# Stage 1 of a hybrid mixer layer: wide products with tokens stationary, and what moves with them

## The chip, the cores and the metric

One NeuronCore of a Trainium2 chip runs one launch of the kernel; all weights and activations are float32 in HBM. The metric is the device time of the launch in microseconds; it is a median of runs. Engines are named TensorE (PE, its weight loads PEld), VectorE (DVE), ScalarE (ACT), GpSimd (POOL) and SyncE (SP).

## The reference

One layer (D = 4096, 256 latent tokens x, 256 context tokens):

```python
shift, scale, gate = split(silu(cvec) @ w_ada + b_ada, 3)     # for c and for c_ctx
h   = rmsnorm(x, norm_w) * (1 + scale) + shift                # x with c, ctx with c_ctx
q, k, v, ga, xl, gl = split(h @ w_in, SPLITS)                 # 2048, 512, 512, 2048, 2048, 2048 columns
att = attention(rope(rmsnorm(q)), rope(rmsnorm(k)), v)        # 16 query heads, 4 key/value heads
u   = conv4(xl) + conv_b
lru = scan_forward(u) + scan_backward(u)                      # context first, then latent tokens; 16 blocks
mix = [rmsnorm(att) * silu(ga), rmsnorm(lru) * silu(gl)]
out = x + gate * (mix @ w_out)                                # latent tokens only
```

Only the latent tokens leave the layer, so of the context just k, v and xl are needed.

## The kernel before, in words

Every large product is computed in three float32r products: an operand is split into a rounded part (hi) and the rest (lo), and hi x hi, hi x lo and lo x hi are summed in PSUM. The weights are split when they arrive: ScalarE copies the high part of a [128, 1024] tile (L640), VectorE subtracts it (L644). The contraction over D runs over 32 k-tiles of 128 rows.

Stage 1 (to about 757 us) makes k, v and xl for both streams. It goes over groups of k-tiles, of 1, 1, 2, 2, 2 and six times 4. For a group it needs shift and scale of the group's channels: `mod_tasks` multiplies silu(c) and silu(c_ctx) by w_ada. Most blocks of four rows go to TensorE (L483; the stationary operand is 32 columns wide, four products side by side in the array), some blocks to VectorE (L470, L472, one multiply-add per row and vector; TensorE folds their sum in, L495). `MOD_V = 6` of the 8 blocks of scale of a full group are on VectorE, none of shift; shift and scale have a bank and a row of their own (L502). `coeff_tasks` sums the row's partitions with products that have the row as stationary operand and two columns moving (L553). `prep_tasks` then transposes the group's tokens (L591), modulates them on ScalarE and splits them (L611).

The group's products follow. `kv_pieces` (L709 to L711) has 128 tokens stationary and 256 weight columns moving; `lru_pieces` (L740) has 128 weight columns stationary and 256 tokens moving, so that xl comes out with channels on partitions. A weight tile of a full group holds four k-tiles by 256 columns. Each filled PSUM bank (four in the pool `pm`) is added to a sum in SBUF by VectorE (L689; L687 for the first group). Per group there are 24 such additions of 512 columns.

Stage 2 makes q (L951 to L953, tokens stationary, 512 columns moving) and the attention, stage 3 the two gates (L975 to L977, weight columns stationary, 256 tokens moving), stage 4 the output projection (L951 to L953 again). Beside stages 2 and 3 the recurrence runs in 16 blocks of 128 channels: xl goes to DRAM after stage 1 (L930), POOL loads a block's gate weights and its xl (L1223, L1225), ScalarE and VectorE make the convolution (L1229, L1232), and gates and scans follow (L1255 to L1257, L1299). Scores, gates, coefficients and some transposes share two PSUM banks (`pe`).

The order of every engine's queue is fixed when the program is built: each piece of work is a task with estimated costs per engine, a due time `pos`, slots that it takes and gives back, and loads; `Plan.order` picks the task that can start first, the most urgent among equals. Engines run their queues in order. The loads of weight tiles go out on SP's queue in the order of their use, through six slots (`raw`).

Of the kernel before, what the change touches and what calls it, by code (L numbers as in the profile page):

```python
# [37 lines left out]
AHEAD = 16.8  # L38
LOAD = 1.500
# [4 lines left out]
QUADS = 1  # L44
LRU_CHUNKS = 10.2
MOD_V = 6
# [11 lines left out]
class Task:  # L58
    """A piece of the program: its engines and their estimated work, and what it waits for."""
# [19 lines left out]

class Plan:  # L80
    """Orders tasks for in-order engines: at each step the task that can start first, the most urgent among equals.
    Slots of the pools are counted, so that the order never needs a slot that is freed only later."""
# [44 lines left out]
    def fixed(self, tasks):  # L127
        """The first tasks, in the order given; their loads are issued as play() does."""
# [13 lines left out]
    def order(self):  # L142
        out, waiting = [], list(self.tasks)
        while waiting:
# [7 lines left out]
            # of the tasks that load, the most urgent of those that could start soon  # L152
# [23 lines left out]
    def put(self, t, s, dma):  # L176
# [6 lines left out]
        for e, c, *table in t.ops:  # L183
            # ScalarE's functions lie in tables, of which one is loaded
            if table and table[0] != self.table:
                self.table = table[0]
                c += TABLE
            s = max(s, self.t[e]) + c
            self.t[e] = s
            s += self.LAT  # L190
        t.end = s - self.LAT
        if t.ops[0][0] == "S":
            # a transfer: it ends later than its issue
            t.end = self.dma = max(self.dma, t.start + 1.3) + t.ops[0][1]
            self.t["S"] = t.start + 0.1
            t.end += 0.9
# [8 lines left out]
def kernel(  # L205
# [34 lines left out]
    SLOTS = dict(h4=(22, 1024), a8=(6, 2048), raw=(RAW, 1024), hi=(HL, 1024), lo=(HL, 1024), tp=(TP, 512), ta=(1, 512), td=(1, 512), wg=(2, 512),  # L240
                 xin=(1, 512), u=(1, 512), ga=(1, 512), ab=(2, 16), mx=(3, 2), ss=(5, 16), pm=(4, 512), pe=(2, 512), pt=(1, 512), po=(1, 512))
# [6 lines left out]
    def slot(cl, shape, dt=F32):  # L248
# [4 lines left out]
        if cl in ROUNDED:  # L253
            # float32r and float32 do not share a tile
# [26 lines left out]
    plan = Plan({cl: n for cl, (n, _) in SLOTS.items() if cl not in ("raw", "td", "ss")} | dict(lh=1, ah=3, lg=1), RAW)  # L281
# [28 lines left out]
    con = cp.tile([128, 130], F32, name="con")  # L310
    ident = con[:, 0:128]
    sel = con[:, 128:130]
# [7 lines left out]
    sc32 = [slot("wg", [128, KT // 2, 32]) for _ in range(2)]  # L320
# [5 lines left out]
    pick = cp.tile([128, 33], F32, name="pick")  # L326
    V.memset(pick, 0.0)
    V.memset(pick[:, 1:2], 1.0)
# [7 lines left out]
    for i in range(2):  # L336
        for v in range(2):
            V.tensor_copy(sc32[i][:, :, v], sc[:, v, KT // 2 * i : KT // 2 * i + KT // 2])
# [65 lines left out]
    def decay():  # L404
        # 4 softplus(-lam) = 4 max(-lam, 0) + 8 atanh(e / (2 + e)), e = exp(-|lam|)
# [18 lines left out]
    def rope_tasks(w, pos, after):  # L424
        """Rotary tables with the norm weights folded in: w * cos, and w with its halves swapped * (-sin | sin)."""
# [21 lines left out]
    def mod_tasks(k0, nk, out_, p0, p1, nb):  # L447
        """silu([c; c_ctx]) @ w_ada for shift and scale of nk k-tiles: partial sums on partitions 32q + vec of a
        row tile; those of some blocks of rows on VectorE, per vec on all partitions."""
# [3 lines left out]
        todo, ends = [], []  # L453
        for part, col0 in enumerate((128 * k0, D + 128 * k0)):
            on_v = MOD_V if part == 1 and nk == G else 0
            v_quads = [(quads * (2 * i + 1)) // (2 * on_v) for i in range(on_v)]
            p_quads = [q for q in range(quads) if q not in v_quads]
            src = w_ada[0, :, col0 : col0 + n].rearrange("(p k) n -> p k n", p=128)
            d = {}

            def on_vector(*w, k, v, first, d=d):
                if v == 0:
                    d["w"] = w[0]
                    if first:
                        d["acc"] = [slot(t, [128, n]) for t in ("xin", "u")]
                a = d["acc"][v]
                for i in range(step):
                    s_ = sc[:, v, k + i : k + i + 1]
                    if first and i == 0:
                        V.tensor_scalar_mul(a, d["w"][:, i], s_)  # L470
                    else:
                        V.scalar_tensor_tensor(out=a, in0=d["w"][:, i], scalar=s_, in1=a, op0=ALU.mult, op1=ALU.add)  # L472
                if v == 1:
                    drop(d["w"])

            cl = "pt" if part else "po"

            def on_tensor(*ws, k, d=d, p_quads=p_quads, cl=cl, on_v=on_v):
                if k == 4 * p_quads[0]:
                    d["ps"] = slot(cl, [128, n])  # L480
                for i in range(step * len(ws)):
                    quad, q = divmod(k + i, 4)
                    T.matmul(  # L483
                        d["ps"][32 * q : 32 * q + 32, :],
# [1048 lines left out]
```

## Time and profile before

| | |
|---|---|
| device time, median of 3 runs | 1804.12 us (1803.67 to 1807.31) |
| profiled execution, first to last instruction | 1805.1 us |
| TensorE / VectorE / ScalarE busy | 1752.0 / 1388.7 / 861.0 us |
| moved by DMA | 452.11 MB, 250 GB/s over the span |

The profiled execution has no other time of its own on record than its span. Busy time of TensorE counts a product from its start to its end, and products overlap: the distance between starts, not the duration of one, is what a product costs in a row of them. PEclk is the share of 2.4 GHz that was granted.

### The profile page before, as it was taken

The page shows a single profiled execution, that of the slowest core. Times are in us where ns is not written, and L with a number is a line of the kernel's source. Part 1 is how long each engine was busy: PE and PEld are TensorE (multiplying, and loading weights), DVE is VectorE, ACT ScalarE, POOL GpSimd, SP SyncE. Part 2 cuts the span into 40 slices and gives each one's busy share as a digit, 9 for nine tenths or more (in the row PEclk, how much of TensorE's full clock was granted, in tenths as well). Part 3 has the DMA queues.
Part 4 walks back from the last instruction along what each step waited for, and adds up shares of the span by engine and source line. Part 5 has one row for each costly group of instructions (what it writes and reads, how often), then busy time and mean ns, then how long its engine had stood idle before and what let it go on. Part 6 is the DMA issues. An engine that isn't in the chain of part 4 may idle for free.

```text
span 1805.1 us, 30493 instructions
## 1 busy us (share of the span) xinstructions
PE 1752.0 (97%) x12093; PEld 1527.8 (85%) x12093; DVE 1388.7 (77%) x1941; ACT 861.0 (48%) x1271; POOL 64.5 (4%) x111
## 2 busy tenths in 40 slices
PE   3999999999999999999999999999999999999998
PEld 2778879888989899977877889999999988888887
DVE  1565988787878797579788886877998997777774
ACT  4422222323232224247787876867776643333332
POOL 2000000000000000110000000000000000000000
PEclk9999999999999999999999999999999999999999
DMA  9989998788887885696555555556777699989883
GB/s 294 329 295 299 311 310 291 265 284 273 262 276 251 293 279 164 225 294 204 182 169 175 181 168 183 176 183 192 237 237 244 208 319 319 316 299 308 303 305 116
DMA packets 304782, 452.11 MB, mean 250 GB/s; under 512 B 15136, under 2 KB 159376, under 8 KB 304128
## 3 DMA queue, kind: packets, MB, share of 16 engines
q1 hardware_dynamic: 297824, 428.43, 71.9%
q0 software_dynamic: 6816, 21.74, 4.2%
q8 instruction: 95, 1.56, 0.4%
q14 instruction: 47, 0.39, 0.1%
HBM read 441.72 MB, written 8.39 MB: 249 GB/s over the span
## 4 chain that ended last, share of the span: by engine, by line
PE 49%; issue 42%; DVE 5%; ACT 2%; DMA 2%; POOL 0%; ACTq 0%; DVEq 0%; POOLq 0%
PE pm L952 8%; PE pm L953 8%; PE pm L951 8%; PE pm L977 6%; PE pm L975 6%; PE pm L976 6%; DVE lo L644 2%; PE po L1141 1%; PE pe L1255 1%; PE pe L1256 1%; PE pe L1257 1%; ACT hi L640 1%; PE pe L1103 1%; DMA rope<-in_q_norm_w_dram 1%; PE pt L1127 0%
## 5 line engine op out<-in xcount | busy, mean ns | idle before, releaser
L640 ACT CAST hi<-raw 128x1024 fp32r<-128x1024 f32 x416 | 434.8, 1047 | 694.9 <-PE pm L953 232.8
L644 DVE TENSOR_TENSOR lo<-raw,hi 128x1024 fp32r<-128x1024 f32 x416 | 506.1, 1221 | 147.7 <-ACT hi L640 140.9
L740 PE MATMUL pm<-h,hi 128*128 128x256 f32 x2048 | 338.8, 288 | 2.8 <-DVE a L689 2.8
L740 PEld LDWEIGHTS pm<-h,hi 128*128 128x128 f32 x2048 | 283.0, 193 | 35.8 <-issue 21.7
L951 PE MATMUL pm<-hi,h 128*128 128x512 f32 x768 | 308.4, 402 | 0.0
L952 PE MATMUL pm<-lo,h 128*128 128x512 f32 x768 | 299.8, 390 | 2.3 <-DVE lo L644 2.3
L953 PE MATMUL pm<-hi,h 128*128 128x512 f32 x768 | 300.2, 391 | 0.0
L975 PE MATMUL pm<-h,hi 128*128 128x256 f32 x1024 | 292.4, 286 | 0.0
L977 PE MATMUL pm<-h,lo 128*128 128x256 f32 x1024 | 289.8, 283 | 1.4 <-DVE lo L644 1.4
L976 PE MATMUL pm<-h,hi 128*128 128x256 f32 x1024 | 289.7, 283 | 0.0
L689 DVE TENSOR_TENSOR a<-pm,a 128x512 f32<-128x512 f32 x240 | 163.0, 687 | 109.0 <-PE pm L740 66.8
L740 PE MATMUL pm<-h,lo 128*128 128x256 f32 x1024 | 206.7, 284 | 0.0
L975 PEld LDWEIGHTS pm<-h,hi 128*128 128x128 f32 x1024 | 196.3, 192 | 1.8 <-issue 0.7
L976 PEld LDWEIGHTS pm<-h,hi 128*128 128x128 f32 x1024 | 196.4, 192 | 1.7 <-issue 0.7
L977 PEld LDWEIGHTS pm<-h,lo 128*128 128x128 f32 x1024 | 196.3, 192 | 1.6 <-DVE lo L644 1.6
L883 DVE SCALAR_TENSOR_TENSOR ga<-raw,sc,ga 128x512 f32<-128x512 f32 x248 | 185.5, 748 | 8.7 <-DMA raw<-in_w_ada_dram 3.9
L952 PEld LDWEIGHTS pm<-lo,h 128*128 128x128 f32 x768 | 144.8, 189 | 34.9 <-DVE lo L644 3.3
L951 PEld LDWEIGHTS pm<-hi,h 128*128 128x128 f32 x768 | 144.7, 188 | 31.3 <-issue 2.9
L953 PEld LDWEIGHTS pm<-hi,h 128*128 128x128 f32 x768 | 144.4, 188 | 30.7
L740 PEld LDWEIGHTS pm<-h,lo 128*128 128x128 f32 x1024 | 160.3, 192 | 0.0
L709 PE MATMUL pm<-hi,h 128*128 128x256 f32 x512 | 151.0, 295 | 1.3 <-ACT h L602 1.3
L710 PE MATMUL pm<-lo,h 128*128 128x256 f32 x512 | 146.0, 285 | 1.0 <-DVE lo L644 1.0
(188 smaller groups left out, 2111.4 us busy)
## 6 DMA issues: line engine op xcount, KB each, us to landing
raw<-in_w_ada_dram SPq DMA_DIRECT2D x384, 512.0 KB, 5.4
raw<-in_w_in_dram SPq DMA_DIRECT2D x288, 512.0 KB, 4.7
raw<-in_w_out_dram SPq DMA_DIRECT2D x128, 512.0 KB, 5.2
h<-in_x_dram SPq DMA_DIRECT2D x8, 512.0 KB, 7.9
h<-in_ctx_dram SPq DMA_DIRECT2D x8, 512.0 KB, 10.9
xl_d<-a POOLq DMA_DIRECT2D x4, 1024.0 KB, 6.5
xin<-xl_d POOLq DMA_DIRECT2D x16, 256.0 KB, 4.4
a<-in_x_dram POOLq DMA_DIRECT2D x8, 512.0 KB, 6.8
```

What stands on the lines that cost most here:

```text
L640: S.copy(d["hi"], raw)
L644: V.tensor_tensor(out=d["lo"], in0=d["raw"], in1=d["hi"].bitcast(F32), op=ALU.subtract)
L689: V.tensor_tensor(out=a, in0=ps, in1=a, op=ALU.add)
L709: T.matmul(o, hi, wh, start=f, stop=False, skip_group_check=True)
L740: T.matmul(d["ps"][:, 256 * j : 256 * j + 256], a, b_, start=f, stop=e, skip_group_check=True)
L883: V.scalar_tensor_tensor(out=d["acc"], in0=w[:, i], scalar=s_, in1=d["acc"], op0=ALU.mult, op1=ALU.add)
L951: T.matmul(ps[t], hi, wh, start=f, stop=False)
L952: T.matmul(ps[t], hi, wl, start=False, stop=False)
L953: T.matmul(ps[t], lo, wh, start=False, stop=e)
L975: T.matmul(o, wh, hi, start=f, stop=False, skip_group_check=True)
L976: T.matmul(o, wh, lo, start=False, stop=False, skip_group_check=True)
L977: T.matmul(o, wl, hi, start=False, stop=e, skip_group_check=True)
```

## The change

All of stage 1 gets 128 tokens stationary and 512 weight columns moving, in one function in place of two. A weight tile of a group with more than one k-tile is two k-tiles by 512 columns. A block of 512 columns fills four banks, one for each stream and token tile, and each is added to the sum in SBUF as before; xl now has tokens on partitions. So each block of the recurrence is loaded from DRAM as [128 tokens, 4 tiles, 128 channels] and turned by four transposes into a bank of `pe`, from which the convolution reads. In the modulation, shift and scale of a group share one bank and one row (columns 0, 1 and 2, 3 of the 32-column operand), and 7 of the 8 scale blocks of a full group are on VectorE. The coefficients come from transposes of the row and a sum over four columns on VectorE. The estimates of the planner change with it: products cost n / 2400 + 0.0136, and due times of stages 2 to 4 follow from that; two constants of the loads' model are other ones.

```diff
-AHEAD = 16.8
-LOAD = 1.500
+AHEAD = 18.0
+LOAD = 1.600
-MOD_V = 6
+MOD_V = (0, 7)
...
+def mm(n, k=1):
+    return k * (n / 2400 + 0.0136)
...
         def sums():
             po = d["po"] = bank()
-            for i, row in enumerate(rows):
-                for j in range(nk):
-                    o, b = 8 * i + 2 * j, slice(128 * j, 128 * j + 128)
-                    T.matmul(po[:, o : o + 2], row[:, b], sel, start=True, stop=True)
-                drop(row)
+            row = rows[0]
+            for j in range(nk):
+                b = slice(128 * j, 128 * j + 128)
+                T.transpose(po[:, b], row[:, b], ident)
+            drop(row)
...
         def fin():
-            pv = d["po"][:, 0:16].rearrange("p (i j v) -> p i j v", i=2, v=2)[:, :, 0:nk]
+            pv = d["po"][:, 0 : 128 * nk].rearrange("p (j q w) -> p j w q", j=nk, q=4)[:, :, 0:4]
+            cf = slot("cf", [128, nk, 4])
+            V.reduce_sum(out=cf, in_=pv, axis=AX.X)
...
+        tiles = [(s, t) for s in ss for t in range(2)]
+        for (name, _), parts in zip(BLOCKS, group_parts[gi]):
+            ps = {}
+            for ip, (u, kk, n, cc, whole) in enumerate(parts):
+                for s, t in tiles:
+                    def mms(s=s, t=t, u=u, kk=kk, n=n, cc=cc, ip=ip, ps=ps, np_=len(parts)):
+                        if ip == 0:
+                            ps[s, t] = bank("pm")
+                        tk = slice(128 * t, 128 * t + 128)
+                        for i in range(n):
+                            g, k = divmod(kk + i, G)
+                            wh, wl = W(u, i, cc, 512)
+                            hi, lo = (x_[:, k, tk] for x_ in (hx, hc)[s][g])
+                            f, e = ip == 0 and i == 0, ip == np_ - 1 and i == n - 1
+                            T.matmul(ps[s, t], hi, wh, start=f, stop=False)
+                            T.matmul(ps[s, t], hi, wl, start=False, stop=False)
+                            T.matmul(ps[s, t], lo, wh, start=False, stop=e)
+                    def done(s=s, t=t, name=name, ps=ps):
+                        accum(acc_tile(name)[:, 2 * s + t], ps[s, t], k0)
+                        drop(ps[s, t])
...
-            d["xin"] = slot("xin", [128, 2, 256])
-            Q.dma_start(d["xin"], xl_d[n // 4, :, n % 4].rearrange("p (s t) -> p s t", s=2))
+            d["xin"] = slot("xin", [128, 4, 128])
+            Q.dma_start(d["xin"], xl_d[n // 4, :, :, 128 * (n % 4) : 128 * (n % 4) + 128])
+        def turn():
+            d["xt"] = bank()
+            for i in range(4):
+                T.transpose(d["xt"][:, 128 * i : 128 * i + 128], d["xin"][:, i], ident)
+            drop(d["xin"])
...
-            S.activation(d["u"], d["xin"], AF.Identity, scale=cvw[2][:, nn], bias=cvb[:, nn])
+            S.activation(d["u"], xt(), AF.Identity, scale=cvw[2][:, nn], bias=cvb[:, nn])
```

## Rows read from the trace of the kernel before

**Rows 1.** The page's shares of the engines, and DMA share in 40 slices

```profile
PE 1752.0 (97%) x12093; PEld 1527.8 (85%) x12093; DVE 1388.7 (77%) x1941; ACT 861.0 (48%) x1271; POOL 64.5 (4%) x111
...
DMA  9989998788887885696555555556777699989883
```

**Rows 2.** Stretches of stage 1: engines' busy us, PEclk, DMA share, GB/s

```profile
45.00:90.00 45.00, 41.44 (x427) 31.85 (x430) 26.70 (x56) 18.63 (x48) 0.00 (x0) 0.92 1.06 329
180.00:225.00 45.00, 45.00 (x365) 38.20 (x365) 41.79 (x61) 13.20 (x19) 0.00 (x0) 1.00 0.92 311
505.30:591.10 85.80, 85.80 (x692) 74.87 (x692) 66.65 (x96) 23.18 (x35) 0.00 (x0) 1.00 0.81 270
549.00:574.00 25.00, 25.00 (x205) 23.23 (x203) 23.24 (x32) 6.65 (x8) 0.00 (x0) 1.00 0.83 284
```

**Rows 3.** Groups of TensorE by form, whole span: line, shapes, count, busy, mean ns

```profile
L740 PE MATMUL pm<-h,hi 128*128 128x256 f32 x2048 | 338.8, 288 | 2.8 <-DVE a L689 2.8
...
L740 PE MATMUL pm<-h,lo 128*128 128x256 f32 x1024 | 206.7, 284 | 0.0
L709 PE MATMUL pm<-hi,h 128*128 128x256 f32 x512 | 151.0, 295 | 1.3 <-ACT h L602 1.3
...
L483 PE MATMUL po<-raw,wg 128*32 128x512 f32 x384 | 54.0, 604 | 1.3 <-DMA raw<-in_w_ada_dram 1.3
...
L483 PE MATMUL pt<-raw,wg 128*32 128x512 f32 x96 | 12.8, 605 | 0.0
```

**Rows 4.** TensorE in order of time, stage 1: start us, us, what

```profile
526.88 0.28 PE L709 MATMUL pm<-hi,h 128*128 128x256 f32 x1
...
528.20 0.28 PE L711 MATMUL pm<-hi,h 128*128 128x256 f32 x1
528.41 1.06 PE L483 MATMUL po<-raw,wg 128*32 128x512 f32 x8
529.40 0.38 PE L709 MATMUL pm<-hi,h 128*128 128x256 f32 x1
...
559.90 0.40 PE L740 MATMUL pm<-h,lo 128*128 128x256 f32 x2
...
560.62 0.40 PE L740 MATMUL pm<-h,lo 128*128 128x256 f32 x2
```

**Rows 5.** The same in the output projection, first and last of 51

```profile
1600.29 0.39 PE L953 MATMUL pm<-hi,h 128*128 128x512 f32 x1
...
1611.62 0.39 PE L952 MATMUL pm<-lo,h 128*128 128x512 f32 x1
```

**Rows 6.** The same around coefficients (L553) and transposes (L591)

```profile
577.14 1.84 PE L553 MATMUL pe<-con,tp 128*128 128x2 f32 x16
578.85 0.72 PE L740 MATMUL pm<-h,hi 128*128 128x256 f32 x4
...
583.24 0.60 PE L591 MATMUL pe<-con,h 128*128 128x128 f32 x4
583.59 0.60 PE L740 MATMUL pm<-h,hi 128*128 128x256 f32 x3
```

**Rows 7.** Groups of VectorE, 45.9 to 757.3 us; the third of the whole span

```profile
L689 DVE TENSOR_TENSOR a<-pm,a 128x512 f32<-128x512 f32 x239 | 162.4, 687 | 109.0 <-PE pm L740 66.8 <-PE pm L711 41.5
...
L472 DVE SCALAR_TENSOR_TENSOR xin<-raw,sc,xin 128x512 f32<-128x512 f32 x138 | 103.3, 748 | 8.6 <-DMA raw<-in_w_ada_dram 6.0
...
L1232 DVE SCALAR_TENSOR_TENSOR u<-xin,parT,u 128x510 f32<-128x510 f32 x32 | 23.9, 746 | 0.6 <-issue 0.3
```

**Rows 8.** Waits of TensorE: us in total, times, longest

```profile
PE pm L740 <- DVE a L689: 2.8, 1, 2.8
```

**Rows 9.** Loads of the recurrence from POOL's queue; landings: the last row's, and a median

```profile
L1225 POOL DMA_DIRECT2D xin<-xl_d x16: 549/549/552, 772.8 to 1341.7; - x16
...
DMA to landing us min/median/max: 3.2/4.4/10.2
...
wg<-in_lru_wa_dram POOLq DMA_DIRECT2D x16, 128.0 KB, 3.6
```

More of the change, by code (lines that the diff above doesn't have):

```diff
@@ new lines, in on_tensor @@
+        def on_tensor(*ws, part, k):
+            if (part, k) == (first_p[0], 4 * first_p[1]):
+                d["ps"] = slot(cl, [128, n])
+            for i in range(step * len(ws)):
+                quad, q = divmod(k + i, 4)
+                half, o = (k + i) // (KT // 2), 32 * ((k + i) % (KT // 2)) + 2 - 2 * part
+                T.matmul(
+                    d["ps"][32 * q : 32 * q + 32, :],
+                    sc32[half][:, o : o + 32],
+                    ws[i // step][:, i % step],
+                    start=(part, quad) == first_p,
+                    stop=(part, quad) == last_p and (q > 1 or last_fold is None),
+                    skip_group_check=True,
+                )
+            drop(*ws)
@@ L454, in mod_tasks, with fold, row @@
+        def fold(part):
+            for v in range(2):
+                o = 3 - 2 * part - v
+                T.matmul(
+                    d["ps"][32 * v : 32 * v + 32, :], pick[:, o : o + 32], d["acc"][v], start=False, stop=part == last_fold, skip_group_check=True
+                )
+            drop(*d["acc"])
+        def row():
+            r = slot("tp", [128, n])
+            S.copy(r, d["ps"])
+            drop(d["ps"])
+            out_.append(r)
         for part, col0 in enumerate((128 * k0, D + 128 * k0)):
-            on_v = MOD_V if part == 1 and nk == G else 0
@@ L456, in mod_tasks @@
-            v_quads = [(quads * (2 * i + 1)) // (2 * on_v) for i in range(on_v)]
-            p_quads = [q for q in range(quads) if q not in v_quads]
+            v_quads = v_of[part]
             src = w_ada[0, :, col0 : col0 + n].rearrange("(p k) n -> p k n", p=128)
[L459 to L484, printed above, removed]
-                        sc32[(k + i) // (KT // 2)][:, (k + i) % (KT // 2)],
-                        ws[i // step][:, i % step],
-                        start=quad == p_quads[0],
-                        stop=quad == p_quads[-1] and (q > 1 or not on_v),
-                        skip_group_check=True,
-                    )
-                drop(*ws)
@@ new lines, in group_pieces @@
+        for (name, _), parts in zip(BLOCKS, group_parts[gi]):
[17 more added lines that the diff above has]
+                        drop(ps[s, t])
+                    end = free and whole and (s, t) == tiles[-1]
+                    last = end and name == "l3" and ip == len(parts) - 1
+                    rel = [lambda g=k0 // G: hc[g]] if last and (k0 + nk) % G == 0 else []
+                    deps = [units[u]["low"]] + [prepared[kk + i, s] for i in range(n)]
+                    p = piece(mms, mm(512, 3 * n), pos, deps, u if end else None, ["pm"] if ip == 0 else [], rel)
+                    pos += mm(512, 3 * n)
+                    if ip == len(parts) - 1:
+                        accum_task(name, done, p, pos)
@@ L799 @@
     p_params = add(load_first_params, [("S", 0.1)])
[L800 removed]
+    ends = mod_tasks(*groups[0], rows0, -100, -90, None, "po")
     mod0 = [t for t in plan.tasks[1:] if t.loads]
```

218 lines of the change are left out of this document (80 added, 138 removed).

## The prediction

> **What bounds the kernel now.** I read the engine shares first, then the stretches, then TensorE's groups and its order in time. TensorE is busy 97% of the span, and the DMA engines are nearly full only in the first eighth and in the last quarter [rows 1]. A busy TensorE is not a TensorE at its best, so the stretches matter more. In the middle of stage 1 the work repeats with a period of 85.8 us for four k-tiles; there TensorE never rests, at full granted clock, VectorE works 66.65 us of it and rests 19.15, and the transfers run at 270 GB/s, where 311 to 329 were reached earlier [rows 2]. So TensorE's instruction stream is the bound in this stage. The early stretches differ: at 45 to 90 us the DMA share is 1.06 and TensorE is short of work, and at 180 to 225 us VectorE is busy 41.79 of 45 us [rows 2].
>
> What the stream pays for shows in the order of time. In the LRU columns six products of 256 columns start within 0.72 us (559.90 to 560.62), so 0.120 us each; in the key/value columns, where tokens already stand still, eleven intervals take 1.32 us (526.88 to 528.20), again 0.120 [rows 4]. In the output projection 50 products of 512 columns take 11.33 us, 0.2266 each [rows 5]. The granted clock is 1.00 there, 2.4 GHz; 256 columns at it are 0.1067 us and 512 are 0.2133, so a product carries about 13 ns on top, whatever its width and whichever operand stands still.
>
> **The change, part by part.**
>
> Wide products. Stage 1 has 3072 LRU products and three times 512 key/value ones, 4608 of 256 columns [rows 3]. They become 2304 of 512: 2304 x (0.2400 - 0.2266) = 30.9 us less, all of it on TensorE's stream, which has no rest to hide in; per four k-tiles 288 x 0.0134 = 3.9. The Trainium skill ("TensorE: Matmul & The Clock Gate", "Back-to-back issue gap") gives a warm gap of N / 2.4 + 2.5 ns; by that this edit would save an estimated 2304 x 2.5 = 5.8 us, not 30.9. The trace does not agree: 13 ns at both widths.
>
> More modulation on VectorE. Each of the six full groups has 16 blocks of four w_ada products; now 10 of them are on TensorE (60 blocks of eight records, 384 + 96 records) [rows 3], after it 9. A block put between two products moves the next one from 0.12 to 1.20 us after the last (528.20 to 529.40), so it costs 1.08 us [rows 4]; six of them are 6.5 us less on TensorE. VectorE gets eight more multiply-adds a group at 0.748 [rows 7], 6.0 us a group and 36 in all. That is hidden as long as VectorE has rest; what it costs without that cover is rival 2.
>
> Coefficients. Sixteen records of tiny products hold TensorE from 577.14 to 578.85, 1.71 us for four k-tiles; four transposes of the same size hold it 0.35 us (583.24 to 583.59) [rows 6]. 8 x 1.36 = 10.9 us less for the 32 k-tiles. There is one row copy on ScalarE instead of two; ScalarE has rest everywhere in stage 1 [rows 2]. VectorE gets one small reduction a group (at most 64 elements a row), which the trace does not show: nothing at the low end, since an added operation gives no time back, and the 0.687 us of a 512-wide sum [rows 7] at the high end. I take 0.2, nearer to nothing by its size; VectorE's rest hides either.
>
> The recurrence turned. 16 blocks get four transposes each, 0.35 us a time [rows 6]: 5.6 us more on TensorE. The convolution then reads PSUM. The three taps of a block take 0.746 us each from SBUF, and the accumulation of 512 columns that reads PSUM takes 0.687 [rows 7], so I count no change for VectorE. The block's load on POOL's queue fetches 512 runs of 512 bytes in place of 128 of 2 KB. Today it lands 4.4 us after its issue (10.2 at worst); a gate weight load of 512-byte runs, half its size, takes 3.6, so twice that, 7.2, is my upper bound for the median and no change the lower one. Its 16 loads are spread over 569 us, 36 us apart [rows 9], so either end is hidden but for the first block. There the wait moves from ScalarE to TensorE: behind the transposes stand the q products. I put 3 us in the range for it and none in the sum.
>
> Weight tiles and banks. In full groups a tile becomes two k-tiles by 512 columns, runs of 2 KB instead of 1 KB on SP's queue, as many bytes and loads as before: no term, a help if anything. But the four PSUM banks now serve one block of columns, and the four sums fall due 1.36 us apart (six products at 0.2266). VectorE, at 0.687 for a sum [rows 7], must free the first bank within three such pieces, 4.1 us; before, a bank was filled by 24 products at 0.120, 2.9 us, and three others lay between, 8.6 us. Two accumulations plus one pair of multiply-adds still fit, so no term, but it bears on rival 2. A group's first products also wait for two prepared k-tiles instead of all four, which may give back a us here and there.
>
> Sum: -30.9 - 6.5 - 10.9 + 5.6 = -42.7 us. Against the span of 1805.1 that is 1762.4. Not all of it can be kept. Some 12 us of it lie before 265 us (8 k-tiles at 0.97 and 12 sets of coefficients at 0.34), where rows 2 show the transfers at 0.92 to 1.06 and VectorE at 41.79 of 45. I keep half of that, between all and nothing. In a full group TensorE's part falls to 85.8 - 3.9 - 1.1 - 1.4 = 79.4 us while VectorE's rises to 66.65 + 6.0 + 0.2 = 72.9, and the transfers must run at 270 x 85.8 / 79.4 = 292 GB/s, under what was reached. Three resources that near each other lose a little in waits: 0.3 us a group, 2 us. This leaves a gain of about 35: 1770 of the span. The span lies 1.0 us over the median of the runs, inside their spread, so I take 1770 for the median too.
>
> **The rivals.**
>
> 1 (my forecast): TensorE stays the bound, 1757 to 1780.
>
> 2: VectorE comes to decide part of stage 1. For it: 72.9 of 79.4 us, and 109.0 us of its rest in stage 1 stand before sums that wait for TensorE [rows 7], rest that its order does not fill. Against it: from 549 to 574 us it works 23.24 of 25 us and TensorE does not rest [rows 2], so it can run this full without harm. If 10 us a group stay unfilled, the period is 82.9 and 21 us are lost: 1784 or so.
>
> 3, the one on the other side: the same rest stays where it is. The order of VectorE's queue is fixed beforehand, a sum stands behind a pair of multiply-adds of 1.5 us, and a bank is now wanted in 4.1 us instead of 8.6. The period is 72.9 plus the rest that stays. It decides from 13.8 us on, where 6 x 7.1 us eat the whole gain; with 16 left of the 19.15 the period is 88.9 and the time 1762.4 + 6 x 9.5 = 1819. Against it: today TensorE's LRU products wait for VectorE's sums a single time, 2.8 us [rows 8].
>
> 4: TensorE stands at the turned blocks. A block keeps one of two shared banks through its three taps, 2.2 us at least [rows 7], and scores and the recurrence's gates use the same two. If TensorE loses half a hold before the transposes and half before the next user of the bank, 16 x 2.2 = 35 us go: 1762.4 + 35 = 1797. With one of the two it is 18 us on top of my 1770: 1788. Against it: the blocks lie far apart and their order is planned.
>
> 5: the 13 ns don't go. If what a product carries grows with its width in stage 1, because weights stand where tokens stood, a wide product costs two narrow ones: the first term falls to nothing and the time is 1801, no change that can be measured. Rows 4 and 5 speak against it in two layouts. The Trainium skill's gap, in the section named above, points the same way and would give an estimated 1795; the trace does not agree with it.
>
> 6: the planner's new due times shift the order of everything and give back the gain: 1804. Nothing speaks for it but that all due times change.
>
> **How the numbers follow.** Chances: forecast 0.60, VectorE in part 0.15, the turned blocks 0.08, the 13 ns kept 0.03, the order 0.04, VectorE's rest kept 0.10. The likeliest gives 1770. The low end is the whole sum with some 5 us more from waits that go (first products that need only two k-tiles): 1757. The high end takes in rivals 2 and 4 and the first block's 3 us: 1797. Left out are rivals 3, 5 and 6 and a little at the low end, not quite 2 in 10. A measurement of this kernel can tell about 0.2%, 3.6 us, from no change. Faster by more than that are cases 1, 2 and 4: 0.83; within it 5 and 6: 0.07; slower rival 3: 0.10.
>
> **What would show it.** Right: products of 512 columns 0.227 us apart in stage 1; a period near 80 us for four k-tiles; VectorE at about 73 of it; stage 1's last product at about 722 us instead of 757; then stages of the same length as before, with some 6 us more where attention and recurrence run. Wrong in rival 2 or 3: TensorE's idle time before stage 1's products ended by VectorE's sums, and VectorE without rest. Wrong in rival 4: idle time of TensorE before the transposes or before scores and gates, ended by taps or by the block's load. Wrong in rival 5: products further apart than 0.227 us. My forecast falls if stage 1 ends later than 740 us, or if the later stages grow by more than 15 us.

## The result, and the profile after

The changed kernel takes **1819.76 us** (median of 4 runs, 1814.42 to 1821.27), the kernel before 1804.17 in the same session: 1.0076 times as long, interval 1.0059 to 1.0093. It is slower by 0.8%, where 1770 was forecast and 1797 was the upper end. The profiled execution took 1821.06 us, 1.9 more than its span of 1819.2.

Where the 14.1 us of span come from shows when the span is cut at the first and last products of each stage (starts of the groups by line; end of stage 1 is the start of its last product):

| stretch, us | before | after | difference | forecast |
|---|---|---|---|---|
| up to stage 1's last product | 757.2 | 744.7 | -12.5 | -40 by the sum |
| query products, to the first gate product | 257.8 | 262.8 | +5.0 | later stages +6 together |
| gate products, to the first of the output | 425.8 | 446.6 | +20.8 | |
| output projection, to the end | 364.3 | 365.1 | +0.8 | |

The groups of products with their first and last start, which give two of the cuts (count, duration ns min/median/max, first to last start us):

```profile
L738 PE MATMUL pm<-hi,h x768: 387/389/797, 41.6 to 744.2; 128*128 128x512 f32 x192
...
L938 PE MATMUL pm<-h,hi x1024: 274/283/682, 1007.5 to 1453.7; 128*128 128x256 f32 x171
```

So two things failed. Stage 1 gives back less than a third of what was summed, and the gate stage, where only the transposes of the turned blocks are new, eats 20.8 us. The page's shares and DMA slices of the changed kernel, which answer to [rows 1]:

```profile
PE 1732.4 (95%) x9709; PEld 1386.6 (76%) x9709; DVE 1419.1 (78%) x2000; ACT 854.8 (47%) x1258; POOL 68.0 (4%) x111
...
DMA  9989988788886975863466447765875798989893
```

TensorE is now busy 95% of a longer span: it has work taken away and idles more. The stretches of stage 1 after, to lay beside [rows 2]; the last row is the gate stage just behind a wait that is shown below:

```profile
45.00:90.00 45.00, 42.35 (x328) 25.52 (x327) 28.65 (x48) 18.72 (x49) 0.00 (x0) 0.96 1.08 338
180.00:225.00 45.00, 45.00 (x223) 30.78 (x222) 43.93 (x65) 13.70 (x19) 0.00 (x0) 1.00 0.94 318
517.70:599.80 82.10, 80.73 (x377) 57.06 (x376) 72.00 (x106) 23.09 (x33) 0.00 (x0) 1.00 0.81 266
...
1334.00:1338.00 4.00, 4.00 (x18) 3.68 (x18) 3.41 (x5) 3.51 (x5) 0.00 (x0) 0.59 0.91 279
```

The early stretches sit against the same two walls as before, a DMA share of 1.08 and 43.93 of 45 us of VectorE. In the full group from 517.7 to 599.8 us VectorE works 72.00 us, as forecast (72.9), but the period is 82.10 and not 79.4, and TensorE, which never rested there before, now rests 1.37.

TensorE's order in the same group, beside [rows 4]:

```profile
523.66 0.39 PE L738 MATMUL pm<-hi,h 128*128 128x512 f32 x1
...
526.83 0.39 PE L740 MATMUL pm<-hi,h 128*128 128x512 f32 x1
527.15 1.07 PE L485 MATMUL pt<-raw,wg 128*32 128x512 f32 x8
528.15 0.50 PE L738 MATMUL pm<-hi,h 128*128 128x512 f32 x1
```

From 523.66 to 526.83 lie 14 intervals of 0.2264 us: wide products run at the forecast price. A block of w_ada products still moves the next product from 0.23 to 1.32 us behind the last, 1.09 more, also the forecast price. What is new stands in the waits. TensorE's largest waits, from 40 to 270 us, from 270 to 760 us, and in the gate stage (us in total, times, longest):

```profile
PE po L485 <- DMA raw<-in_w_ada_dram: 4.2, 1, 4.2
PE pt L485 <- DMA raw<-in_w_ada_dram: 4.1, 5, 1.3
PE pm L740 <- DVE h L617: 3.5, 1, 3.5
PE pm L738 <- DVE a L695: 3.1, 5, 1.4
...
PE pm L738 <- DVE a L695: 5.7, 6, 1.7
PE pt L485 <- DMA raw<-in_w_ada_dram: 2.8, 3, 1.5
PE po L485 <- DMA raw<-in_w_ada_dram: 2.4, 4, 1.0
...
PE pe L1228 <- DVE lo L1220: 10.0, 6, 2.5
```

In the kernel before, the view is empty from 270 to 760 us, and the gate stage has one wait of 1.4 us and one of 0.6. From 40 to 270 us it has these two as its largest:

```profile
PE po L483 <- DMA raw<-in_w_ada_dram: 4.9, 5, 2.0
PE pm L740 <- DVE a L689: 2.8, 1, 2.8
```

Adding up stage 1 from each product's start to the next start, by line, gives the account: wide products 583.7 us before, 574.8 after (-8.9, -30.9 forecast); w_ada's products 100.0 and 105.2 (+5.2, -6.5 forecast); coefficients 13.6 and 2.8 (-10.8, -10.9 forecast). The waits that the view names from 40 to 760 us add up to 29.3 us where they were 10.4. By groups of k-tiles, from the first product of one to that of the next: the first 8 k-tiles took 224.9 us before and 224.6 after, so nothing came of the change there; the six full groups took 492.3 and 478.5. In the same way the gate stage's 20.8 are 13.4 in the recurrence's gate products (30.7 before, 44.1 after), 3.9 for 44 new transposes, 4.1 at the narrow gate products, and -0.6 for the rest.

One of the six waits of the gate stage, in order of time on VectorE and TensorE:

```profile
1315.45 1.22 DVE L650 TENSOR_TENSOR lo<-raw,hi 128x1024 fp32r<-128x1024 f32 x1
1316.58 0.41 DVE L1342 SCALAR_TENSOR_TENSOR ta<-ta,pm 128x256 f32<-128x256 f32 x1
...
1323.62 1.53 DVE L846 SCALAR_TENSOR_TENSOR ga<-raw,sc,ga 128x512 f32<-128x512 f32 x2
1325.08 1.22 DVE L650 TENSOR_TENSOR lo<-raw,hi 128x1024 fp32r<-128x1024 f32 x1
...
1329.13 3.11 DVE L846 SCALAR_TENSOR_TENSOR ga<-raw,sc,ga 128x512 f32<-128x512 f32 x4
1332.15 0.69 DVE L1219 TENSOR_TENSOR lo<-wg,hi 128x512 fp32r<-128x512 f32 x1
1332.76 0.69 DVE L1220 TENSOR_TENSOR lo<-u,hi 128x512 fp32r<-128x512 f32 x1
...
1330.57 0.39 PE L1227 MATMUL pe<-hi 128*128 128x512 f32 x1
1333.50 0.50 PE L1228 MATMUL pe<-lo,hi 128*128 128x512 f32 x1 [2.54 <-DVE lo L1220]
...
1335.02 0.41 PE L939 MATMUL pm<-h,hi 128*128 128x256 f32 x1
...
1335.87 0.41 PE L940 MATMUL pm<-h,lo 128*128 128x256 f32 x1
```

VectorE does not rest here: the low half of a recurrence block (L1220) stands behind four multiply-adds of the gate vector (L846, 3.02 us) and is done 2.5 us after TensorE has reached the product that needs it (L1228). Both queues are fixed beforehand; TensorE came too early in its own.

### The profile page after: what moved, and what is told of

It reads as the page before. It is cut to its first block, busy times and chain, and to the rows that moved or that the text cites. A ratio compares the mean times of both kernels' runs of the same rounds, so it can differ in the third digit from the quotient of the medians.

```text
span 1819.2 us, 25705 instructions
## 1 busy us (share of the span) xinstructions
PE 1732.4 (95%) x9709; PEld 1386.6 (76%) x9709; DVE 1419.1 (78%) x2000; ACT 854.8 (47%) x1258; POOL 68.0 (4%) x111
## 4 chain that ended last, share of the span: by engine, by line
issue 43%; PE 39%; DVE 12%; ACT 3%; DMA 2%; POOL 0%; DVEq 0%; ACTq 0%; POOLq 0%
PE pm L915 8%; PE pm L916 8%; PE pm L914 8%; DVE lo L650 4%; PE pm L939 4%; PE pm L938 4%; PE pm L940 4%; DVE ga L846 2%; PE po L1104 1%; ACT hi L646 1%; DVE h L1270 1%; DVE h L1271 1%; PE pe L1066 1%; DVE u L1204 1%; PE pt L1090 1%
## 5 line engine op out<-in xcount | busy, mean ns | idle before, releaser
L738 PE MATMUL pm<-hi,h 128*128 128x512 f32 x768 | 316.5, 412 | 10.9 <-DVE a L695 8.7
L914 PE MATMUL pm<-hi,h 128*128 128x512 f32 x768 | 308.5, 402 | 0.0
L740 PE MATMUL pm<-hi,h 128*128 128x512 f32 x768 | 302.2, 394 | 3.5 <-DVE h L617 3.5
L739 PE MATMUL pm<-lo,h 128*128 128x512 f32 x768 | 302.0, 393 | 0.8 <-DVE lo L650 0.8
L915 PE MATMUL pm<-lo,h 128*128 128x512 f32 x768 | 299.7, 390 | 1.6 <-DVE lo L650 1.6
L916 PE MATMUL pm<-hi,h 128*128 128x512 f32 x768 | 299.4, 390 | 0.0
L938 PE MATMUL pm<-h,hi 128*128 128x256 f32 x1024 | 293.7, 287 | 0.0
L940 PE MATMUL pm<-h,lo 128*128 128x256 f32 x1024 | 290.7, 284 | 0.8 <-DVE lo L650 0.8
L939 PE MATMUL pm<-h,hi 128*128 128x256 f32 x1024 | 290.2, 283 | 0.0
L738 PEld LDWEIGHTS pm<-hi,h 128*128 128x128 f32 x768 | 145.4, 189 | 104.0 <-issue 41.0
L939 PEld LDWEIGHTS pm<-h,hi 128*128 128x128 f32 x1024 | 197.0, 192 | 1.7 <-issue 0.7
L938 PEld LDWEIGHTS pm<-h,hi 128*128 128x128 f32 x1024 | 196.9, 192 | 1.7 <-issue 0.7
L940 PEld LDWEIGHTS pm<-h,lo 128*128 128x128 f32 x1024 | 196.8, 192 | 1.4 <-DVE lo L650 1.4
L846 DVE SCALAR_TENSOR_TENSOR ga<-raw,sc,ga 128x512 f32<-128x512 f32 x248 | 185.8, 749 | 8.1 <-DMA raw<-in_w_ada_dram 3.2
L740 PEld LDWEIGHTS pm<-hi,h 128*128 128x128 f32 x768 | 145.5, 189 | 36.0 <-DVE h L617 3.9
L915 PEld LDWEIGHTS pm<-lo,h 128*128 128x128 f32 x768 | 144.4, 188 | 35.0 <-DVE lo L650 3.5
L914 PEld LDWEIGHTS pm<-hi,h 128*128 128x128 f32 x768 | 144.3, 188 | 31.3 <-issue 3.1
L916 PEld LDWEIGHTS pm<-hi,h 128*128 128x128 f32 x768 | 144.1, 188 | 30.4
L739 PEld LDWEIGHTS pm<-lo,h 128*128 128x128 f32 x768 | 145.7, 190 | 27.2 <-DVE lo L650 1.3
```

The lines of the kernel that those rows point to most:

```text
L738: T.matmul(ps[s, t], hi, wh, start=f, stop=False)
L739: T.matmul(ps[s, t], hi, wl, start=False, stop=False)
L740: T.matmul(ps[s, t], lo, wh, start=False, stop=e)
L846: V.scalar_tensor_tensor(out=d["acc"], in0=w[:, i], scalar=s_, in1=d["acc"], op0=ALU.mult, op1=ALU.add)
L914: T.matmul(ps[t], hi, wh, start=f, stop=False)
L915: T.matmul(ps[t], hi, wl, start=False, stop=False)
```

## The experiments

All sixteen, with what the trace shows of the two stages in question ("last" is the start of stage 1's last product, "gates" the length of the gate stage). The median of the kernel before was 1804.72 to 1805.62 us in these sessions. The stages are read from one profiled execution each. In stage 1 the changed kernel, e5 and e15 have the same TensorE order and end it at 744.7, 741.9 and 741.0 us; e3, e6, e9 and e10, but for one tie, at 739.1, 739.1, 741.3 and 736.5. Differences of up to 5 us between stage ends are thus not clear of the spread.

| run | kernel | last | gates | us, median | ratio, interval |
|---|---|---|---|---|---|
| | before (profile) | 757.2 | 425.8 | 1804.17 | |
| | after (profile) | 744.7 | 446.6 | 1819.76 | 1.0076 (1.0059 to 1.0093) |
| e1 | after, VectorE's planned costs up | 760.6 | 429.8 | 1820.24 | 1.008 (1.0053 to 1.0107) |
| e2 | after, old planned cost of products | 753.2 | 428.9 | 1808.4 | 1.002 (1.001 to 1.0029) |
| e3 | after, 6 blocks on VectorE | 739.1 | 443.0 | 1813.12 | 1.0045 (1.003 to 1.006) |
| e4 | before, new planned cost of products | 767.2 | 441.2 | 1834.76 | 1.0166 (1.0151 to 1.0182) |
| e5 | after, old cost behind stage 1 only | 741.9 | 428.9 | 1795.62 | 0.9946 (0.9931 to 0.996) |
| e6 | e5, 6 blocks | 739.1 | 428.9 | 1793.37 | 0.994 (0.992 to 0.996) |
| e7 | e5, 5 blocks | 743.2 | 428.9 | 1797.64 | 0.9957 (0.9942 to 0.9972) |
| e8 | after, half of VectorE's w_ada work | 730.7 | 444.7 | 1804.8 | 1.0 (0.9989 to 1.0011) |
| e9 | e6, due times old, clock new | 741.3 | 444.7 | 1818.33 | 1.007 (1.0051 to 1.0089) |
| e10 | e6, due times new, clock old | 736.5 | 429.6 | **1791.22** | **0.9922** (0.9907 to 0.9936) |
| e11 | e6, old constants of loads | 743.6 | 430.9 | 1796.76 | 0.9945 (0.9926 to 0.9964) |
| e12 | e6, 7 load slots | 758.2 | 428.9 | 1814.54 | 1.005 (1.0032 to 1.0067) |
| e13 | after, half of w_ada's bytes | 723.7 | 444.5 | 1800.96 | 0.9976 (0.9966 to 0.9985) |
| e14 | both halves | 710.6 | 443.7 | 1788.09 | 0.9908 (0.9892 to 0.9925) |
| e15 | after, gate multiply-adds' cost up | 741.0 | 442.0 | 1815.46 | 1.0058 (1.0039 to 1.0076) |
| e16 | after, VectorE's general cost up | 759.0 | 433.2 | 1819.42 | 1.0074 (1.0055 to 1.0092) |

### The planner's costs, from both sides (e1, e2, e4), and VectorE's load (e3)

e1, in the changed kernel:

```diff
-    return k * (0.07 + n / 962)
+    return k * (0.157 + n / 960)
-[("D", 1.33)]
+[("D", 1.50)]
```

> The changed kernel with VectorE's costs in the planner put to what its trace shows: 0.157 us + n / 960 instead of 0.07 + n / 962, and 1.50 instead of 1.33 us for a pair of gate multiply-adds; the work itself is the same, its order is another. Theory M (mismatch): the change made the planner's product costs right and left VectorE's about 11% short, so that TensorE reaches VectorE's results too early; then this kernel gives back most of the 20.8 us that the gate stage grew (446.6 towards 428 us), its waits at the recurrence's second gate product fall from 11 to under 3 us, stage 1 ends near 735 instead of 745 us, and the time is about 1795, 0.995 of the kernel before. Theory L (load): what costs is the load itself (VectorE at 72 of 80 us a group, the turned blocks and their bank); then the order changes little and the time stays within 0.3% of the changed kernel, 1.005 to 1.011.

e2, in the changed kernel (`mm`, the planned cost of wide and of later products):

```diff
-    return k * (n / 2400 + 0.0136)
+    return k * n / 2400
```

> The changed kernel with the planner's product cost put back to n / 2400 without the 13.6 ns; the work is the same. Theory M: TensorE is again planned about as much too fast as VectorE, the two errors cancel, and the gate stage's waits at the recurrence's gates go: about 1798, 0.997. Theory L: within 0.3% of the changed kernel, 1.005 to 1.011.

e3, in the changed kernel:

```diff
-MOD_V = (0, 7)
+MOD_V = (0, 6)
```

> The changed kernel with 6 instead of 7 scale blocks of a full group on VectorE. TensorE gets 6 x 1.08 = 6.5 us more, VectorE 36 us less. Theory L: VectorE's and the transfers' waits in stage 1 shrink by more than that, stage 1 ends by 740 us, and the time falls to 1810 or less (1.003). Theory M: the waits stay, stage 1 ends between 745 and 752 us and the time is 1815 to 1827 (1.006 to 1.013).

e4, in the kernel before (`pe`, and a gate piece's cost as 12 products of 256):

```diff
-    return k * n / 2400
+    return k * (n / 2400 + 0.0136)
```

> The kernel before with the 13.6 ns a product in the planner's costs, as the change has them, and nothing else; the work is the same. Theory M: the kernel before gets slower by itself, above all in the gate stage (425.8 us towards 440), about 1815, 1.006. Theory L: no difference above 0.2%, 0.998 to 1.002.

The medians alone tell little, since the parts go against each other; the stages tell. Both e1 and e2 bring the gate stage back to 429 us, by opposite edits: one makes VectorE slower in the planner's eyes, the other TensorE faster. e4 puts the gate stage's loss into the kernel before, with none of the change's instructions: 425.8 to 441.2. So 17.7 of the gate stage's 20.8 us are made by the planner's estimates (446.6 to 428.9 in e2, with the lower clock behind two of the waits, which the last section shows); the 3.1 that stay are about the 3.9 of the new transposes. The recurrence's wait comes with the estimate in e4, too, at the same product, which is L1256 there:

```profile
PE pe L1256 <- DVE lo L1248: 7.3, 6, 2.1
```

In stage 1 the same two edits do harm (760.6 and 753.2 for 744.7), where e1 was expected near 735; so the medians miss theory M's 1795 and 1798. The new cost of products is not better for stage 1 as such: in the kernel before it makes stage 1 10.0 us longer (e4). e3 takes back what the change added to VectorE's modulation: stage 1's last product comes 5.6 us earlier, though TensorE gets six blocks of 1.09 us back. VectorE's load seems to cost more there than the blocks did, but 5.6 us is hardly more than the spread. The whole of e3, 1813.12 us, lies between what theories L and M asked.

### The parts put together (e5, e6, e7)

e5, in the changed kernel; e6 and e7 set MOD_V to (0, 6) and (0, 5) as well:

```diff
-    U2, U3 = mm(512, 12), mm(256, 24)
+    U2, U3 = pe(512, 12), pe(256, 24)
```

> The changed kernel with the old cost of a product (no 13.6 ns) in the query, gate and output stages only; stage 1 keeps the new cost and the 7 blocks on VectorE. Theory P (the loss behind stage 1 is made by the planner's new due times and costs of the gate products, and by nothing in stage 1): the end of stage 1 stays at 744.7 us, the gate stage goes from 446.6 to about 429 us, the query stage from 262.9 to 258, the whole to about 1798 us (ratio 0.996). Theory S (the gate stage is long because stage 1 leaves it late accumulations and loads, so that it was the old order of stage 1 that helped in the second experiment): the gate stage stays at 440 us or more, the whole at 1812 or more.

> As the run before it, with 6 blocks of weight rows on VectorE in place of 7. Theory P, with the two faults adding up: 739.1 + 258 + 429 + 364.5 = about 1790.5 us of span and 1792 us in all, 0.993 of the kernel before, so faster than both kernels. Theory S: the stage behind takes back what stage 1 gains, 1803 or more.

> As the run before it, with 5 blocks on VectorE: one more block of 16 products per full group goes to TensorE (6 times 3.3 us = 20 us of work at most) and leaves VectorE (6 times 6 us = 36 us). Theory V (VectorE's load sets the pace of stage 1 in the changed kernel): stage 1 ends below 739, near 733, because one block fewer gave 5.6 us already; the whole near 1786. Theory T (TensorE sets it from 6 blocks on): stage 1 ends at 739 to 755, the whole 1792 to 1808.

Theory P holds: stage 1 keeps its gain, the gate stage is 428.9 us long, and the kernel is faster than the kernel before and the changed one, 0.9946 and 0.994. The later stages of e5 take 4.1 us more than before the change, where some 6 were forecast. With 5 blocks stage 1 ends at 743.2 and the median is 1797.64, inside what theory T says (from 6 blocks on it is TensorE that pays). But seven, six and five blocks lie within 4.1 us of each other in stage 1, so theory T is not shown; theory V's 733 is out.

### Due times or the planner's clock (e9, e10)

The number of the products enters the planner twice: through due times, and through the time by which its clock of TensorE moves when a piece is placed. e9 and e10 part the two, on e6; e9:

```diff
-                    ends[t] = piece(mms, U2 / 2, units[u]["pos"] + t * U2 / 2, [units[u]["low"]] + deps(g), u if t == 1 else None,
+                    ends[t] = piece(mms, mm(512, 6), units[u]["pos"] + t * U2 / 2, [units[u]["low"]] + deps(g), u if t == 1 else None,
...
-                    ends[h] = piece(mms, U3 / 2, units[u]["pos"] + m * U3 / 2, [units[u]["low"]], u if m == 1 else None,
+                    ends[h] = piece(mms, mm(256, 12), units[u]["pos"] + m * U3 / 2, [units[u]["low"]], u if m == 1 else None,
```

e10 has U2, U3 by `mm`, and `pe(512, 6)`, `pe(256, 12)` in the pieces.

> The sixth experiment's kernel (6 blocks on VectorE, old cost behind stage 1), but the pieces of 6 and of 12 products behind stage 1 carry the new cost in the planner's clock; their due times keep the old pace. It tells apart which half of the planner's number lost the 18 us of the gate stage. Theory P1 (the due times, spread 13% wider than the chip's pace needs against the recurrence's own): the gate stage stays at 429 us and the whole at about 1793. Theory P2 (the planner's clock, in which a gate product now lasts longer while VectorE's steps stay 11% too short, so that recurrence products are queued ahead of the VectorE work that they need): the gate stage is 441 to 447 us and the whole about 1806 to 1811.

> The other half: due times behind stage 1 at the new pace, the planner's clock at the old cost. Theory P1: gate stage 441 to 447 us, the whole 1806 to 1811. Theory P2: 429 us and about 1793.

Theory P2: the cost in the planner's clock makes the gate stage's loss (444.7 and 429.6 us). The whole of e9 missed, 1818.33 us where 1806 to 1811 were expected; its query stage grew as well, to 267.3 us from 258.7 in e6. The waits of the gate stage's stretch (1000 to 1450 us) in e9 have the recurrence's wait again:

```profile
PE pe L1228 <- DVE lo L1220: 5.4, 3, 3.2
PE pt L1039 <- DVE tp L974: 2.3, 2, 1.2
```

and in e10 (994 to 1423.8 us) two short ones are all that is left:

```profile
PE pm L940 <- DVE lo L650: 0.6, 2, 0.4
PE pt L1090 <- DVE tp L1084: 0.4, 1, 0.4
```

Of the kernels that do all the work e10 is the fastest, 1791.22 us; against e6 (1793.37) its interval overlaps.

### A false number of VectorE, or slack (e15, e16)

The expectations of e1 and e9 have VectorE's planned steps 11% too short. The rows of the gate stage's wait say otherwise: a subtraction of 1024 columns moves the next instruction by 1.13 us (1315.45 to 1316.58), and the planner has 1.134. The 1.22 in the row is the instruction's own duration, which overlaps the next. What is short in the planner, of the steps in these rows, is the pair of gate multiply-adds, 1.46 us in the trace (1323.62 to 1325.08) against 1.33. e15 sets that one to 1.50 and e16 the general one to 0.157 + n / 960, which is now too long; the diffs are the two halves of e1's.

> The changed kernel with the planner's cost of a pair of the gate vector's multiply-adds at 1.50 us in place of 1.33; nothing else. In the trace such pairs start 1.46 us apart in the gate stage. Theory N (one VectorE number was false, and a true TensorE number laid it bare): the gate stage falls from 446.6 to about 430 us and the whole to about 1803. Theory K (no VectorE number matters by itself: the order needs slack at VectorE, which a TensorE taken as too fast had given): the gate stage stays at 440 or more.

> The changed kernel with the planner's general VectorE cost raised from 0.07 + n / 962 to 0.157 + n / 960 us, which is longer than the trace's distance of starts (1.13 to 1.14 us for 1024 columns, which the old number meets with 1.134); the gate vector's multiply-adds stay at 1.33. Theory K: the gate stage falls to about 430 us although the number is now false. Theory N: it stays at 440 or more. Stage 1 ends at about 760 us in both, as in the first experiment, because the general number is what moved it there.

The true correction brings 4.6 us of the gate stage back, the false one 13.4; together they brought 16.8 in e1. So theory K for the larger part: what the order lacks is slack. The planner places a recurrence product on TensorE where it computes that VectorE will be done, with 0.15 us for the hand-over (`LAT`) and no other margin. With a piece of 12 gate products at 1.28 us, where the chip takes 12 x 0.120 = 1.44 [rows 4], the planner's TensorE runs ahead of the true one, and the product lands some pieces later in the queue. The number that is true of TensorE took that margin away. TensorE's waits at this product (L1228) in the gate stage follow: 10.0 us in the changed kernel, 9.8 in e3, 5.4 in e9, 4.9 in e15, 1.4 in e16, 0.6 in e1 and none in e2, e5, e6, e7 and e10. That the margin is the reason, and not some other property of these orders, is inferred from the orders that have it (e1, e2, e5 to e7, e10, e16) and those that have not (the changed kernel, e3, e4, e9); a margin by itself wasn't tried.

### What keeps stage 1 (e8, e13, e14)

e8 takes half of VectorE's w_ada work away and leaves the order as it is:

```diff
                 if first and i == 0:
                     V.tensor_scalar_mul(a, d["w"][:, i], s_)
-                else:
+                elif v == 0:
                     V.scalar_tensor_tensor(out=a, in0=d["w"][:, i], scalar=s_, in1=a, op0=ALU.mult, op1=ALU.add)
```

> The changed kernel with VectorE's products for the second modulation vector left out (7 blocks times 4 rows, each first row's multiply kept: 27 of 56 instructions of 0.746 us per full group, 20 us of some 73 busy us in a group of 80); the order of all that is left, TensorE's products and the loads are as they were. What it leaves out is the most part of the context's shift-and-scale sums on VectorE. Theory V (VectorE's load keeps stage 1 at 744.7): stage 1 ends near 722, as forecast, groups of 78 to 80 us. Theory R (w_ada's and the weights' transfers, or the order itself, keep it): stage 1 ends at 738 or more. The gate stage stays at 440 to 447 in both.

e13 halves the bytes (and so in `on_vector` `i // 2`, in `on_tensor` `i % step // 2`):

```diff
-[([128, step, n], src[:, kk : kk + step])
+[([128, step // 2, n], src[:, kk : kk + step // 2])
```

> The changed kernel with every load of w_ada's shift and scale halved (half of the rows are loaded, each is used twice; the modulation is computed from these); the order, the instructions of TensorE and VectorE and their sizes are as in the changed kernel. 32 of 56 or so loads of a full group carry half their bytes. Theory R (the transfers' own time makes w_ada late): the waits for w_ada, 16 us up to 760 us, go to under 3 us and stage 1 ends at 728 to 735 in place of 744.7. Theory V (VectorE frees the slots late, so that loads are asked for late): waits shrink by under 5 us, stage 1 ends at 740 or more. The gate stage stays at 443 to 447 us.

e14 has both.

> Both halves: half the bytes of w_ada's loads, and VectorE's products for the second modulation vector left out (with half of VectorE's part alone, stage 1 ended at 730.7). If transfers and VectorE together are all that kept stage 1 from the forecast, it ends at 720 to 724. If it ends at 728 or more, what is left is neither: TensorE's own cost at the change between w_ada's narrow products and the wide ones, the clock, or the order.

With fewer bytes the first group also begins 8 us earlier, so I read stage 1 from its first to its last start of L738. In e8:

```profile
L738 PE MATMUL pm<-hi,h x768: 387/389/796, 39.4 to 730.2; 128*128 128x512 f32 x192
```

In e13:

```profile
L738 PE MATMUL pm<-hi,h x768: 387/389/795, 33.6 to 723.3; 128*128 128x512 f32 x192
```

In e14:

```profile
L738 PE MATMUL pm<-hi,h x768: 387/389/717, 33.3 to 710.1; 128*128 128x512 f32 x192
```

That is 702.6 us in the changed kernel, 690.8 with less VectorE, 689.7 with fewer bytes, 676.8 with both: -11.8, -12.9, and -25.8, about the sum of the two. Theory V and theory R each hold in part: neither 722 us in e8 nor 740 in e13 came. e14 went past its 720 to 724: 710.6 us, of which 8 are the earlier begin. From first to last product it is 40.4 us shorter than the 717.2 of the kernel before, as much as the forecast's sum asked of the change, with the changed kernel's order on TensorE. The waits fit. In e13 only one wait for w_ada is left from 40 to 760 us, 1.4 us, where the changed kernel has 13.5; the waits for VectorE's sums stay, 11.9 us for 8.7. In e8 no wait for w_ada is left from 270 us on:

```profile
PE pm L738 <- DVE a L695: 5.9, 3, 2.3
PE pm L915 <- DVE lo L650: 1.1, 1, 1.1
```

so the early ones (8.7 us in e8 up to 270 us, 8.3 in the changed kernel) hang on the transfers. The late ones go with either half, so they seem to have needed both: long transfers, and slots that VectorE freed late. Both halves take away more than the change had added (27 x 0.749 = 20 us a group of VectorE, against 6), so they show which resources bind, not how many of the missing us belong to each. Nor do they show what another order of the same work would give back: e1, e2, e4 and e16, which change nothing but the order, move stage 1's end by 8 to 16 us, all of them to a later end; a search for a better one wasn't made.

### Two ways that led nowhere (e11, e12)

e11, on e6:

```diff
-AHEAD = 18.0
-LOAD = 1.600
+AHEAD = 16.8
+LOAD = 1.500
```

> The sixth experiment's kernel with the load model's two numbers (how far ahead of its products a weight tile is wanted, 18.0, and the length of a load, 1.6) set back to 16.8 and 1.5. If these made w_ada's blocks wait for their transfers (6.7 us behind 270 us in the sixth experiment, 0.85 before the change), stage 1 ends 4 to 6 us earlier, at 733 to 735; if late slots (VectorE) made them, stage 1 stays at 737 to 742 and the whole within 3 us of 1793.

e12, on e6 (its other slot is given up in `h4`, 22 to 21, for the memory):

```diff
-RAW = 6
+RAW = 7
```

> The sixth experiment's kernel with 7 slots for loaded weights in place of 6 (one of 22 other slots of the same size given up for it). A load is asked for when a slot is free, and slots are freed by VectorE's subtraction or by w_ada's products. If slots are what makes w_ada's blocks late, the 8.5 us of waits for w_ada go to under 3 and stage 1 ends near 733, the whole near 1787. If the transfers' own rate is (338 GB/s in the early groups), only the later groups gain, under 3 us, and the early waits stay. The slot given up may cost some us where the attention or the recurrence runs; then the stages behind grow and stage 1 still tells.

No loss by the constants of the loads' model shows: with the old ones stage 1 ends 4.5 us later, not 4 to 6 earlier, and the runs spread from 1790.25 to 1799.98 us. e12 says little. The waits for w_ada up to 270 us went from 4.4 us in e6 to 0.3, so the early loads may gain from a slot, but those behind grew (5.9 us for 3.0), and with the slot given up came a new wait that costs more than all of this:

```profile
PE pe L597 <- ACT h L608: 12.9, 9, 2.1
```

The preparation of the tokens, whose tiles lie in those slots, comes late. What seven slots are worth without that price stays open.

## Why the prediction was wrong, point by point

- **The clean prices held.** Wide products are 0.2264 us apart, so rival 5 is out. The Trainium skill ("TensorE: Matmul & The Clock Gate", "Back-to-back issue gap") has N / 2.4 + 2.5 ns, which it calls the gap of an isolated product, an estimated 0.2158 here; the trace does not agree after the change either. Coefficients gave 10.8 us of 10.9. The 64 transposes of the recurrence take 6.0 us from start to next start, for 5.6. The taps cost 745 ns from PSUM, 746 from SBUF before, and the blocks' loads land after 4.6 us, 6.2 at worst, inside the bounds of 4.4 and 7.2. TensorE waits 0.3 us in all before the turned blocks, and 0.3 us once for a tap that held the scores' bank, so rival 4 is out.
- **"I keep half of that ... 2 us" was the step that failed in stage 1.** The wide products kept 8.9 of 30.9 us and w_ada's blocks turned -6.5 into +5.2; that is 33.7 us short, where the text took 8 off, 6 of them for the first 8 k-tiles. There nothing was kept at all (224.9 and 224.6 us), and the full groups, which should have given 38 less 2, gave 13.8. Each of the two limits, transfers and VectorE, was seen in [rows 2] and judged one at a time, by its mean over a group: 72.9 of 79.4 us, 292 GB/s under 329. As a mean VectorE's came out right (72.00 us), and the transfers ran at 266 GB/s; neither is a limit by itself. But the order is rigid, and resources that are busy for eight to nine tenths of the period meet TensorE's queue at fixed places: waits of up to 4.2 us at w_ada's loads and up to 1.7 at the sums. Lightening VectorE gave 11.8 us, the transfers 12.9, both 25.8 (e8, e13, e14). Rival 2 named VectorE's half of it; the transfers' half had no rival.
- **The later stages' "some 6 us more" came out at 26.6, and the step that failed there is rival 6.** It was given 0.04 with the remark that nothing spoke for it. The cost of products in `mm` stood in the diff, and the text priced every instruction but not the planner's estimate. It was also not the due times, as rival 6 had it, but the cost in the planner's clock of TensorE (e9, e10): with the old cost behind stage 1 the 26.6 fall to 4.1 (e5). One part of rival 6 fits: it gives back the whole gain.
- **Rival 3, the one on the other side,** gave 1819 us, and 1819.76 was measured. That is chance. VectorE's rest in a full group is 10.1 us (82.10 - 72.00), not 16, and 20.8 us were lost in a stage of which rival 3 says nothing.
- **Slips in the sums:** stage 1 ending at 722 us and 6 us more behind it make 1776, not 1770; the sum itself asked for 717. Rival 3 decides from 13.6 us on, not 13.8, and 16 loads over 569 us are 38 us apart, not 36. None of these bears on the outcome. Both signs by which the forecast was to fall came: stage 1 ended after 740 us, and the later stages grew by more than 15.

Without the estimate's effect the change is what it was meant to be, at little over a quarter of the size: e5 gains 9.3 us (1804.91 - 1795.62) where 35 were forecast.

## What to carry to other kernels

When a kernel's order is computed from estimates, a change of an estimate is a change of every queue: it is a part of the change with a price of its own, and a truer number can make a worse order, here most likely since the error had served as a margin. Change it by stage, and cut the trace by stage before reading any total. And where a saving on the bound engine brings two other resources to eight or nine tenths of the new period, a fixed order can lose most of it, as stage 1 did.

## What the runs showed of the hardware

**A wait of 2.5 us can cost more than its length, and need not.** After TensorE had stood 2.54 us at L1228, the granted clock was 0.59 from 1334 to 1338 us, where it was 1.00 from 1325 to 1330 us, before the wait, and 0.99 again from 1338 to 1342; in the row of that stretch above only 18 products lie in 4 us. Between 1335.02 and 1335.87 us five narrow products start, 0.2125 us apart, which is the lower level of 1.2 GHz, against 0.120 at the full clock. The twelve narrow products behind this wait, from 1334.81 to 1337.37 us, took 2.56 us where 1.44 is the price at the full clock: 1.1 us on top of the wait. In e3 the same product waits as long, and the stretch behind it is at the full clock (a row of the order in time, and one of the stretches):

```profile
1326.18 0.50 PE L1228 MATMUL pe<-lo,hi 128*128 128x512 f32 x1 [2.54 <-DVE lo L1220]
...
1326.00:1330.00 4.00, 3.82 (x22) 3.42 (x23) 3.93 (x6) 3.01 (x5) 0.52 (x1) 1.00 0.97 314
```

Of the changed kernel's six waits at L1228 the lower clock followed on two (2.38 and 2.54 us); in e3 the same two were followed by none, and its gate stage is 3.6 us shorter, 443.0 for 446.6. What decides it these runs don't show.

**The 13 ns are gone at the lower clock, at 256 columns.** 256 columns at 1.2 GHz are 0.2133 us, all of the distance that the rows show; at 2.4 GHz they are 0.1067 of 0.120. The Trainium skill ("TensorE: Matmul & The Clock Gate", "Back-to-back issue gap") states N / 1.2 GHz with nothing on top for the cold array; the trace agrees there.
